# A state space scan turned by phases and scanned in hardware, in place of a tree of complex products

## Chip, cores and metric

The kernel runs on one core of one Trainium2 chip. The metric is the device time of one execution in microseconds (us). Engines: PE (TensorE), DVE (VectorE), ACT (ScalarE), POOL (GpSimd), SP (SyncE). Each engine works through its own instructions in the order in which the program gives them, and waits at the head of its queue for semaphores of the others.

## What is computed

Two transformer blocks on 256 positions of 1024 channels. The second block has a state space branch (S5), an mLSTM branch and a retrieval layer (PEER). The change is in the state space branch alone:

```python
lam = lax.complex(a_re, a_im)
dt = jnp.exp(log_dt)[:, None]
a_bar = jnp.exp(lam * dt)
b_bar = ((a_bar - 1.0) / lam)[..., None] * lax.complex(b_re, b_im)
bu = jnp.einsum('blgc,gpc->blgp', u, b_bar)
a_seq = jnp.broadcast_to(a_bar, (1, L) + a_bar.shape)
def combine(e1, e2):
    a1, b1 = e1
    a2, b2 = e2
    return a1 * a2, a2 * b1 + b2
_, states = lax.associative_scan(combine, (a_seq, bu), axis=1)
y = jnp.real(jnp.einsum('blgp,gcp->blgc', states, c)) + d * u
```

So there is a complex recurrence x[t] = a x[t-1] + bu[t] for each of 32 x 64 states. The kernel takes four positions at a time: with 272 positions there are 68 steps, and the factor of a step is a to the fourth power.

## The kernel before

Weights come through one stream of units of 8 tiles (128x128). For each unit, ACT rounds it into `wh` (line 338), DVE subtracts for the rest `wl` (line 339), and PE does three matmuls for each tile (lines 408 to 410, or 435 to 437 for the z part with 512 columns). Both splits run up to three units ahead of PE (`enter`, line 321); `wh` and `wl` have four buffers each.

All other work is written as generators that `tick` (line 369) steps between units, by a table of costs that each `yield` gives. A scheduler then fixes the order on every engine.

- `_prep` (line 479) runs during the feed forward part of the first block. It computes the step factor on tiles of 16 columns with DVE, and squares it eight times into `pw` (lines 637 to 643): 6 instructions of the helper `cmul` (lines 564 to 569) and one more (line 640) for each square. `expand` (line 503) makes block diagonal matrices on POOL.
- `_block2` (line 668) is the second block up to the retrieval layer. `ssm` (line 746) brings the inputs into `u4` and multiplies them with `ew` into `z2` (real and imaginary part, 16 groups, 68 steps; PE line 769, ACT line 771). Then comes the tree: `step` (line 778) does four DVE instructions for each of six levels up and five or six down, all at line 786. Its reads and writes skip: level i touches every 2, 4, 8, ... steps. Then `py` (lines 809 and 812) takes the states to the output.
- `memory` (line 844) is the mLSTM branch. After a convolution on DVE (line 851) it calls `expand` twice for each of eight column blocks e (lines 862 and 863): one matrix for the keys (buffer e % 2) and one for the values (one buffer). PE multiplies by them: `pk` (line 866) and `pv` (line 873). ACT takes both out of PSUM (lines 867, 875, 876). At the end come the gates: `pg` (line 883), a chain through ACT and DVE over the small tile `GR` (lines 885 to 892), and the matmul `pf` (line 895).
- Meanwhile the main stream of PE is `us`, `xm` (8 units), `z` (8 units), then `g` (16 units); DVE takes each `g` out of PSUM at line 1013, ACT applies tanh at line 1014.

The call that ends the preparation stands at line 1973 (`K.finish(prep)`). `paced` (line 355) makes an instruction be issued after the last product on POOL at line 1951.

Of the kernel before, what the change touches and what calls it, by code (L numbers as in the profile page):

```python
# [14 lines left out]
ALU = mybir.AluOpType  # L15
# [240 lines left out]
def _bc(ap, axis, n):  # L256

    v = ap.unsqueeze(axis)
    shape = list(v.shape)
    shape[axis] = n  # L260
    return v.to_broadcast(shape)
# [217 lines left out]
def _prep(K, dump):  # L479

    nc, I, cols = K.nc, K.I, K.cols
    g = nc.gpsimd
    act, mm, tp = nc.scalar.activation, nc.tensor.matmul, nc.tensor.transpose
    tt, ts, stt = nc.vector.tensor_tensor, nc.vector.tensor_scalar, nc.vector.scalar_tensor_tensor
    EW, CX, TT, ZZ, BX = (K.big(f"s5{i}") for i in range(5))
    ew = EW.a(16, 2, 64)
    cx = [CX.a(16, 4, 16) for _ in range(2)]
    tz = TT.a(16, 64)
    u4 = TT.a(16, 68)
    pw = TT.a(9, 48)  # L490
    z2, tmp = ZZ.a(2, 16, 68), ZZ.a(1088)
    M5 = K.big("ml5")
    mp, nqk = M5.a(513), M5.a(32)
    nc.scalar.dma_start(mp, I["mlp"])
    fold = TT.a(2, 8, 8)
    ex = M5.a(3, P)
    msk = mp[:, 481:513]
    wif = mp[:, 288:480].rearrange("p (a b) -> p a b", b=8)
# [3 lines left out]

        g.tensor_tensor(dst.rearrange("p (a b) -> p a b", b=4), _bc(w[:, 4 * e:4 * e + 4], 1, 32), _bc(msk, 2, 4), ALU.mult)

    K.s5 = ew, cx, tz, z2, tmp, pw, u4
    K.mlf = TT, M5, mp, nqk, wv, fold, ex, expand

    raw = ZZ.t[:, 0:1328]
# [13 lines left out]
        yield 0.1  # L522
    v = [sc[:, i] for i in range(32)]
    dt, rho, th, n, r, sn, cs_, hs, den, kr, ki, u, w = v[:13]
    act(dt, ld, AF.Exp)
    tt(rho, lr, dt, ALU.mult)
    tt(th, li, dt, ALU.mult)
# [11 lines left out]
    act(hs, r, AF.Sin, scale=0.5)  # L539
    tt(hs, hs, hs, ALU.mult)  # L540
    ts(cs_, hs, -2.0, 1.0, ALU.mult, ALU.add)
    ar, ai = pw[:, 8, 0:16], pw[:, 8, 32:48]
    tt(ar, rho, cs_, ALU.mult)
    tt(ai, rho, sn, ALU.mult)
    yield 0.4
# [17 lines left out]
    def cmul(dr, di, xr_, xi, yr, yi, a, b, f):  # L563
        f(a, xr_, yr, ALU.mult)
        f(b, xi, yi, ALU.mult)
        f(dr, a, b, ALU.subtract)
        f(a, xr_, yi, ALU.mult)
        f(b, xi, yr, ALU.mult)
        f(di, a, b, ALU.add)
# [59 lines left out]
    a, b = outputs(), inputs()  # L629
    while True:  # L630
        c, d = next(a, None), next(b, None)
# [1 line left out]
            break  # L633
        yield (c or 0) + (d or 0)

    pr, pi_ = ar, ai
    for i in range(8):
        qr, qi = pw[:, i, 0:16], pw[:, i, 32:48]
        cmul(qr, qi, pr, pi_, pr, pi_, u, w, tt)
        ts(pw[:, i, 16:32], qi, -1.0, None, ALU.mult)  # L640
        pr, pi_ = qr, qi
        if i % 2:
            yield 0.5

    pr4 = ZZ.t[:, 3648:3776]
    v3 = lambda z: z.rearrange("p (e j d) -> p e j d", j=4, d=4)
# [3 lines left out]
    for n in range(10):  # L650
# [8 lines left out]
        v = pf[:, 0:32].rearrange("p (a e b) -> p a e b", a=2, e=2)  # L659
# [8 lines left out]
def _block2(K, X, eps, dump, stop):  # L668
    nc, I, cols = K.nc, K.I, K.cols
    g = nc.gpsimd  # L670
# [1 line left out]
    tt, ts, stt = nc.vector.tensor_tensor, nc.vector.tensor_scalar, nc.vector.scalar_tensor_tensor  # L672
    scopy, vcopy = nc.scalar.copy, nc.vector.tensor_copy
    xr = X[:, :, NM:]
    ew, cx, tz, z2, tmp, pw, u4 = K.s5
    y4 = tmp[:, 0:1024].rearrange("p (a b) -> p a b", a=16)
    TT, M5, mp, nqk, wv, fold, ex, expand = K.mlf

# [67 lines left out]
    def ssm():  # L746

        yield 0.1
        du = K.dram.tile([P, 1088], F32, name="du")
        nc.scalar.dma_start(du, us.rearrange("p n t j -> p (n t j)"))  # L750
        yield 0.1
        d = du.rearrange("(r e c) (n t j) -> e t c n r j", r=4, e=2, n=4, t=4)
        for e in range(2):
            for t in range(4):
                z = 64 * e + 16 * t
                nc.scalar.dma_start(u4[z:z + 16].rearrange("c (n r) j -> c n r j", r=4), d[e, t])
        yield 0.1
        yield 0.1

        for q0 in range(0, 16, 6):  # L760
            ps = []
            for q in range(q0, min(q0 + 6, 16), 3):
                n = min(3, 16 - q)
                p = K.pm_("pe")
                ps.append((q, n, p))
                for j in range(n):
                    for i in range(2):
                        for z in halves:
                            mm(p[z, (i * n + j) * 68:(i * n + j + 1) * 68], ew[z, q + j, i], u4[z, q + j], start=True, stop=True)
            for q, n, p in ps:  # L770
                scopy(z2[:, :, q:q + n], p[:, 0:2 * n * 68].rearrange("p (i a b) -> p i a b", i=2, a=n))
            yield 0.1
        K.bg.sort(key=[sc, ml_, res].index)
        K.e_done = True

        lv = [1, 2, 4, 8, 16, 32]

        def step(i, dst, src):
            z0, zx, z1 = z2[:, :, :, src], z2[:, ::-1, :, src], z2[:, :, :, dst]
            n = z0.shape[3]  # L780
            t = tmp[:, 0:32 * n].rearrange("p (a b c) -> p a b c", a=2, b=16)
            re = _bc(_bc(pw[:, i + 1, 0:16], 1, 2), 3, n)
            im = _bc(pw[:, i + 1, 16:48].rearrange("p (a b) -> p a b", a=2), 3, n)
            c = 0.06 + n * 32 / 960
            for x, y, w, op in ((t, z0, re, ALU.mult), (z1, z1, t, ALU.add), (t, zx, im, ALU.mult), (z1, z1, t, ALU.add)):
                tt(x, y, w, op)  # L786
                spent[0] += c
                if spent[0] > 1.0:
                    yield spent[0]
                    spent[0] = 0.0  # L790

        spent = [0.0]
        N = 68
        for i, d in enumerate(lv):
            m = len(range(2 * d - 1, N, 2 * d))
            if m:
                yield from step(i, slice(2 * d - 1, N, 2 * d), slice(d - 1, d - 1 + 2 * d * (m - 1) + 1, 2 * d))
        for i, d in reversed(list(enumerate(lv))):
            m = len(range(3 * d - 1, N, 2 * d))
            if m:  # L800
                yield from step(i, slice(3 * d - 1, N, 2 * d), slice(2 * d - 1, 2 * d - 1 + 2 * d * (m - 1) + 1, 2 * d))

        for h in range(2):
            p = K.pm_("py")
            for j in range(8):
                q = 8 * h + j
                o = p[:, j * 64:(j + 1) * 64]
                for z in halves:
                    mm(o[z], tz[z, q], u4[z, q, 4:], start=True, stop=False)
                for i in range(2):  # L810
                    for z in halves:
                        mm(o[z], cx[i][z, q].rearrange("p a b -> p (a b)"), z2[z, i, q, 3:67], start=False, stop=i == 1)
            act(y4[:, 8 * h:8 * h + 8], p.rearrange("p (a b) -> p a b", a=8), AF.Gelu_apprx_tanh)
            yield 0.1
        dy = K.dram.tile([P, 1024], F32, name="dy")
        nc.scalar.dma_start(dy, tmp[:, 0:1024])
        yield 0.1
        yt = yv.rearrange("p n (t j) -> p n t j", t=4)
        d = dy.rearrange("(e t c) (n r j) -> r e c n t j", e=2, t=4, n=4, r=4)
        for r in range(4):  # L820
            for e in range(2):
                z = 32 * r + 16 * e
                nc.scalar.dma_start(yt[z:z + 16], d[r, e])
        yield 0.1
        K.R1 = K.big("s5r", F32R)
        K.yh, K.yl = K.R1.a(4, T1), K.R1.a(4, T1)
        K.split(K.yh, K.yl, yv)
        yield 1.1
# [548 lines left out]
def trainium_kernel(ctx, tc, I, O, dump=None, stop=None):  # L1377
# [591 lines left out]
    for i in range(NFF - 3):  # L1969
        up(i)  # L1970
        if i >= DN:
            down(i - DN)
    K.finish(prep)

    with K.behind():
        nc.scalar.dma_start(meta, I["metaT"])
# [57 lines left out]
```

## Time and profile before

| | |
|---|---|
| three runs, median | 1530.45 us (1529.59 to 1530.96) |
| the profiled execution | 1530.96 us; its span 1529.2 us |
| PE busy | 1501.1 us, 98% of the span |
| DVE busy | 1138.1 us, 74% |
| ACT busy | 832.0 us, 54% |
| POOL busy | 237.2 us, 16% |
| granted TensorE clock, mean of the span | 0.995 of full speed |
| second block up to the retrieval layer | about 486 us to 720 us of the span |

Read it like this: PE is busy almost all the time, so other engines matter only where PE waits for them. The list of waits of PE names those places; the timeline of an engine in such a stretch shows what held it up.

### The profile page before, as it was taken

The numbers are of one execution on the slowest core, as the hardware profiler recorded it, in microseconds if no ns is written. First come the engines' busy times: TensorE is split into PE (matmuls) and PEld (weight loads), VectorE is DVE, ScalarE is ACT, GpSimd is POOL, SyncE is SP. The second block draws the span as 40 slices with busy tenths as digits, with TensorE's granted clock in tenths as the row PEclk, the third lists the DMA queues.
The fourth block names the chain that finished last, engine by engine and source line by source line (L and its number), as shares of the span: only waits on it lengthen the run. The fifth ranks groups of instructions, "written<-read, shape, count | busy, mean of one in ns | idle before, by whom it ended". The sixth has DMA issues, their size and how long they took to land.

```text
span 1529.2 us, 30332 instructions
## 1 busy us (share of the span) xinstructions
PE 1501.1 (98%) x11917; PEld 1403.6 (92%) x11917; DVE 1138.1 (74%) x2167; ACT 832.0 (54%) x1442; POOL 237.2 (16%) x257
## 2 busy tenths in 40 slices
PE   8999999999999998999999999999999999999998
PEld 7999899999999987999999999999999888888886
DVE  6865666886867796677989888888998666666664
ACT  7745445775455565665554455555445555555554
POOL 1000000267330020001100522222332000000000
PEclk9999999999999998999999999999999999999999
DMA  7543344555554533446455455554555555555553
GB/s 271 169 136 112 99 150 166 190 197 163 153 179 163 176 114 123 132 159 209 139 184 187 152 177 172 177 160 157 168 165 178 195 193 193 193 193 193 193 194 109
DMA packets 81439, 257.37 MB, mean 168 GB/s; under 512 B 17809, under 2 KB 19601, under 8 KB 81169
## 3 DMA queue, kind: packets, MB, share of 16 engines
q1 hardware_dynamic: 69344, 247.32, 49.2%
q10 hardware_dynamic: 11952, 8.13, 1.7%
q8 instruction: 93, 1.52, 0.4%
q14 instruction: 50, 0.40, 0.1%
HBM read 252.96 MB, written 2.13 MB: 167 GB/s over the span
## 4 chain that ended last, share of the span: by engine, by line
PE 84%; DVE 10%; POOL 2%; issue 2%; ACT 2%; DMA 1%; SPq 0%; ACTq 0%; DVEq 0%; POOLq 0%
PE acc L1340 23%; PE U L408 7%; PE U L410 7%; PE U L409 7%; DVE wl L339 3%; PE g L408 3%; PE g L410 3%; PE g L409 3%; PE u L410 3%; PE u L408 2%; PE u L409 2%; PE pG L1220 2%; DVE s L786 1%; PE acc L1965 1%; PE acc L1963 1%
## 5 line engine op out<-in xcount | busy, mean ns | idle before, releaser
L339 DVE TENSOR_TENSOR wl<-wr,wh 128x1024 fp32r<-128x1024 f32 (+1 forms) x469 | 584.2, 1248 | 196.4 <-ACT wh L338 191.9
L338 ACT CAST wh<-wr 128x1024 fp32r<-128x1024 f32 (+1 forms) x469 | 490.8, 1048 | 387.1 <-PE U L409 144.9
L1340 PE MATMUL acc<-wh,wring 128*128 128x512 f32 x1024 | 315.6, 389 | 0.0
L408 PE MATMUL U<-hh,wh 128*128 128x256 f32 x1024 | 289.8, 283 | 0.0
L410 PE MATMUL U<-hh,wl 128*128 128x256 f32 x1024 | 288.1, 281 | 1.5 <-DVE wl L339 1.4
L409 PE MATMUL U<-hl,wh 128*128 128x256 f32 x1024 | 288.3, 282 | 0.0
L1340 PEld LDWEIGHTS acc<-wh,wring 128*128 128x128 f32 x1024 | 192.2, 188 | 40.0
L1340 PE MATMUL acc<-wl,wring 128*128 128x512 f32 x512 | 199.2, 389 | 0.0
L410 PEld LDWEIGHTS U<-hh,wl 128*128 128x128 f32 x1024 | 193.9, 189 | 1.9 <-DVE wl L339 1.9
L408 PEld LDWEIGHTS U<-hh,wh 128*128 128x128 f32 x1024 | 193.6, 189 | 0.0
L409 PEld LDWEIGHTS U<-hl,wh 128*128 128x128 f32 x1024 | 192.4, 188 | 0.0
L1331 ACT ACTIVATE wring<-act 128x256 fp32r<-128x256 f32 x128 | 53.3, 418 | 149.7 <-PE acc L1340 147.1
L1340 PEld LDWEIGHTS acc<-wl,wring 128*128 128x128 f32 x512 | 96.1, 188 | 19.9
L1301 POOL TENSOR_TENSOR act<-act,ga 128x16 f32<-128x16 f32 (+31 forms) x77 | 74.9, 972 | 191.9 <-ACT ga L1300 170.4
L1332 DVE SCALAR_TENSOR_TENSOR wring<-act,wring 128x256 fp32r<-128x256 f32 x128 | 54.7, 428 | 61.3 <-PE acc L1340 58.9
L410 PE MATMUL u<-hh,wl 128*128 128x256 f32 x320 | 89.9, 282 | 3.3 <-DVE wl L339 3.3
L408 PE MATMUL u<-hh,wh 128*128 128x256 f32 x320 | 90.3, 284 | 0.2 <-ACT hh L440 0.2
L409 PE MATMUL u<-hl,wh 128*128 128x256 f32 x320 | 89.7, 281 | 0.0
L455 POOL TENSOR_TENSOR sq<-sq,sq 128x256 f32<-128x256 f32 x18 | 16.0, 889 | 404.6 <-ACT sq L451 404.4
L408 PE MATMUL g<-hh,wh 128*128 128x256 f32 x256 | 73.7, 288 | 0.0
L409 PE MATMUL g<-hl,wh 128*128 128x256 f32 x256 | 72.0, 281 | 0.0
L410 PE MATMUL g<-hh,wl 128*128 128x256 f32 x256 | 71.9, 281 | 0.0
(639 smaller groups left out, 3309.2 us busy)
## 6 DMA issues: line engine op xcount, KB each, us to landing
wr<-in_W SPq DMA_DIRECT2D x211, 512.0 KB, 3.5
wr<-in_U SPq DMA_DIRECT2D x128, 512.0 KB, 3.8
wr<-in_V SPq DMA_DIRECT2D x128, 512.0 KB, 4.3
tkc<-in_keysT ACTq DMA_DIRECT2D x1, 1024.0 KB, 6.2
wsA<-in_cst ACTq DMA_DIRECT2D x1, 804.0 KB, 6.8
s<-in_s5p ACTq DMA_DIRECT2D x1, 664.0 KB, 4.7
wsA<-in_rows ACTq DMA_DIRECT2D x1, 640.0 KB, 5.5
du<-ml ACTq DMA_DIRECT2D x1, 544.0 KB, 2.7
```

The lines of the kernel that those rows point to most:

```text
L338: a = nc.scalar.copy(hi[:, q], raw[:, q])
L339: b = nc.vector.tensor_tensor(lo[:, q], raw[:, q], hi[:, q].bitcast(F32), ALU.subtract)
L408: mm(out, wh, ah, start=first, stop=False)
L409: mm(out, wh, al, start=False, stop=False)
L410: self.last = mm(out, wl, ah, start=False, stop=last).ins
L455: self.nc.gpsimd.tensor_tensor(self.part[0], self.part[0], s, ALU.add)
L786: tt(x, y, w, op)
L1220: mm(o, r[:, k, :, e % 2], r[:, 4 + 2 * w + k, :, e % 2], start=w == 0, stop=w == 1)
L1301: g.tensor_tensor(d[:, :n], d[:, :n], a[:, :n], ALU.mult)
L1331: act(hi, w, AF.Copy, scale=1.0 / 16384)
L1332: stt(lo, w, 1.0 / 16384, hi.bitcast(F32), ALU.mult, ALU.subtract)
L1340: mm(acc[t][c], w[:, q], v[:, 4 * c:4 * c + 4].rearrange("p a b -> p (a b)"), start=False, stop=i == NE - 1 and len(vs) == 1, skip_group_c ...
```

## The change

Write x[t] = e[t] s[t], where e[t] is the phase of the step factor to the power t (modulus one). Then s obeys a real recurrence, s[t] = r s[t-1] + conj(e[t]) bu[t], with r the modulus of the factor. DVE has an instruction for that (`tensor_tensor_scan`). So the inputs are turned back by their phases, scanned as real and imaginary part, and turned forward again. The table of phases `er`, `ei` (16 groups, 68 steps) is built on POOL by doubling in `phases`, which is called behind the end of the preparation; `r4` holds the modulus for every step, with 0 at the first of a group so that one scan runs over many groups. Groups 0 to 9 are turned on DVE, groups 10 to 15 (`rest`) on POOL.

```diff
-    pw = TT.a(9, 48)
-    z2, tmp = ZZ.a(2, 16, 68), ZZ.a(1088)
+    a1 = TT.a(2, 16)
+
+    er, ei = EW.a(16, 68), CX.a(16, 68)
+    z2, tmp = ZZ.a(2, 16, 68), ZZ.a(1920)
...
+    r4 = TT.a(16, 68)
...
-    pr, pi_ = ar, ai
-    for i in range(8):
-        qr, qi = pw[:, i, 0:16], pw[:, i, 32:48]
-        cmul(qr, qi, pr, pi_, pr, pi_, u, w, tt)
-        ts(pw[:, i, 16:32], qi, -1.0, None, ALU.mult)
-        pr, pi_ = qr, qi
-        if i % 2:
-            yield 0.5
+    cmul(step[0], step[1], cs_, sn, cs_, sn, u, w, tt)
+    cmul(er[:, :, 1], ei[:, :, 1], step[0], step[1], step[0], step[1], u, w, tt)
+    tt(step[2], rho, rho, ALU.mult)
+    tt(step[2], step[2], step[2], ALU.mult)
+    yield 1.5
+
+    def phases():
+        g.memset(er[:, :, 0:1], 1.0)
+        g.memset(ei[:, :, 0:1], 0.0)
+        for m in (1, 2, 4, 8, 16, 32, 64):
+            k = min(m, 67 - m)
+            x = [ZZ.t[:, o:o + 16 * k].rearrange("p (a b) -> p a b", a=16) for o in (1328, 3136)]
+            d, y = slice(m + 1, m + 1 + k), slice(1, 1 + k)
+            cmul(er[:, :, d], ei[:, :, d], er[:, :, y], ei[:, :, y], _bc(er[:, :, m], 2, k), _bc(ei[:, :, m], 2, k), *x, g.tensor_tensor)
+        nc.scalar.copy(r4, _bc(step[2], 2, 68))
+        g.memset(r4[:, :, 0:1], 0.0)
+
+    K.phases = phases
...
-        lv = [1, 2, 4, 8, 16, 32]
-
-        def step(i, dst, src):
-            z0, zx, z1 = z2[:, :, :, src], z2[:, ::-1, :, src], z2[:, :, :, dst]
-            n = z0.shape[3]
-            t = tmp[:, 0:32 * n].rearrange("p (a b c) -> p a b c", a=2, b=16)
-            re = _bc(_bc(pw[:, i + 1, 0:16], 1, 2), 3, n)
-            im = _bc(pw[:, i + 1, 16:48].rearrange("p (a b) -> p a b", a=2), 3, n)
-            c = 0.06 + n * 32 / 960
-            for x, y, w, op in ((t, z0, re, ALU.mult), (z1, z1, t, ALU.add), (t, zx, im, ALU.mult), (z1, z1, t, ALU.add)):
-                tt(x, y, w, op)
...
+        def turn(e, q, j, back, buf):
+            z = z2[:, :, q, j]
+            n, m = z.shape[2], z.shape[3]
+            t = buf[:, :2 * n * m].rearrange("p (a b c) -> p a b c", a=2, b=n)
+            e.tensor_tensor(t, z2[:, ::-1, q, j], _bc(ei[:, q, j], 1, 2), ALU.mult)
+            e.tensor_tensor(z, z, _bc(er[:, q, j], 1, 2), ALU.mult)
+            yield 0.1 + n * m * 4 / 960
+            for i in range(2):
+                e.tensor_tensor(z[:, i], z[:, i], t[:, i], ALU.add if i == back else ALU.subtract)
+            yield 0.1 + n * m * 2 / 960
+
+        def scan(q):
+            flat = lambda z: z[:, q].rearrange("p a b -> p (a b)")
+            for i in range(2):
+                z = flat(z2[:, i])
+                nc.vector.tensor_tensor_scan(z, flat(r4), z, 0.0, ALU.mult, ALU.add)
+                yield 0.1 + z.shape[1] * 2.3 / 960
+
+        all_, out, rest = slice(0, 68), slice(3, 67), slice(10, 16)
+        for _ in turn(g, rest, all_, 0, tmp[:, 1024:]):
+            pass
+        for q in (slice(0, 5), slice(5, 10)):
+            yield from turn(nc.vector, q, all_, 0, tmp)
+        for q in (slice(0, 10), rest):
+            yield from scan(q)
+        for _ in turn(g, rest, out, 1, tmp[:, 1024:]):
+            pass
+        for q in (slice(0, 5), slice(5, 8), slice(8, 10)):
+            yield from turn(nc.vector, q, out, 1, tmp)
...
     K.finish(prep)
+    with K.paced():
+        K.phases()
```

In the changed file the lines behind the edits are shifted: `expand` is line 506 there, the two products of `turn` are lines 794 and 795, its two sums line 798, the scan line 805, and the tanh and the take-out of `g` lines 1031 and 1030.

The order on POOL in the second block, before: the matrices of `expand` (line 503, tile `ml`) stand alone, after two memsets. The first three of the sixteen stand further ahead.

```order
L878 MEMSET GR 128x272 [waits PE_49]
L923 MEMSET ml_6562 128x384 [waits Activation_49,Pool_49]
L503 TENSOR_TENSOR ml_3403<-ml_3403 128x128 [waits PE_49] x3
L503 TENSOR_TENSOR ml_3403<-ml_3403 128x128 [waits PE_49,Pool_49]
L503 TENSOR_TENSOR ml_3403<-ml_3403 128x128 [waits PE_49]
L503 TENSOR_TENSOR ml_3403<-ml_3403 128x128 [waits PE_49,Pool_49]
```

The same place now (`expand` is line 506; the tiles `s` are the states, the phases and the scratch tile):

```order
L895 MEMSET GR 128x272 [waits PE_49]
L940 MEMSET ml_6571 128x384 [waits Activation_49]
L794 TENSOR_TENSOR s_3401<-s_3401,s_3399 128x816 [waits Activation_49,Pool_49]
L795 TENSOR_TENSOR s_3401<-s_3401,s_3398 128x2x408 [waits Pool_49]
L798 TENSOR_TENSOR s_3401<-s_3401 128x408 [waits Pool_49]
L798 TENSOR_TENSOR s_3401<-s_3401 128x408
L506 TENSOR_TENSOR ml_3403<-ml_3403 128x128 [waits PE_49] x3
L506 TENSOR_TENSOR ml_3403<-ml_3403 128x128 [waits PE_49,Pool_49]
L794 TENSOR_TENSOR s_3401<-s_3401,s_3399 128x768 [waits DVE_49]
L795 TENSOR_TENSOR s_3401<-s_3401,s_3398 128x2x6x64 [waits Pool_49]
L506 TENSOR_TENSOR ml_3403<-ml_3403 128x128 [waits PE_49]
L798 TENSOR_TENSOR s_3401<-s_3401 128x6x64 [waits Pool_49]
```

Ahead of the four matrices (values of e = 1, keys of e = 2, values of e = 2, keys of e = 3) now stands the turn back of groups 10 to 15. Ahead of the fifth (values of e = 3) stand the two products of the turn forward, which wait for DVE.

What they wait for on DVE is the last of the four scans (line 805). It stands here, with the splits of the weight stream (line 339) between:

```order
L798 TENSOR_TENSOR s_3401<-s_3401 128x340 x2
L339 TENSOR_TENSOR wl_6657<-wr_6533,wh_6656 128x1024
L805 SCALAR_TENSOR_TENSOR s_3401<-s_3400,s_3401 128x680 x2
L805 SCALAR_TENSOR_TENSOR s_3401<-s_3400,s_3401 128x408
L339 TENSOR_TENSOR wl_6691<-wr_6580,wh_6690 128x1024
L805 SCALAR_TENSOR_TENSOR s_3401<-s_3400,s_3401 128x408
L794 TENSOR_TENSOR s_3401<-s_3401,s_3399 128x640
```

Before, the tree (line 786) stood in this place and reached much further down: its last instruction stood behind line 892, now the last turn on DVE stands ahead of line 888 (905 in the changed file).

On DVE in the preparation, before, the stretch between two splits:

```order
L566 TENSOR_TENSOR s_3400<-s_3400 128x16
L567 TENSOR_TENSOR s_3400<-s_3400 128x16
L568 TENSOR_TENSOR s_3400<-s_3400 128x16
L569 TENSOR_TENSOR s_3400<-s_3400 128x16
L640 TENSOR_SCALAR s_3400<-s_3400 128x16
L1948 SCALAR_TENSOR_TENSOR ffn_3005<-u_4739,cols,ffn_3005 128x255
L1949 SCALAR_TENSOR_TENSOR ffn_3005<-u_4739,cols,ffn_3005 128x254
L339 TENSOR_TENSOR wl_4780<-wr_4590,wh_4779 128x1024
```

and now the same stretch:

```order
L339 TENSOR_TENSOR wl_4742<-wr_4523,wh_4741 128x1024
L661 TENSOR_TENSOR s_3401<-ml_3403 128x128
L662 TENSOR_REDUCE ml_3403<-s_3401 128x32
L1965 SCALAR_TENSOR_TENSOR ffn_3005<-u_4739,cols,ffn_3005 128x255
L1966 SCALAR_TENSOR_TENSOR ffn_3005<-u_4739,cols,ffn_3005 128x254
L339 TENSOR_TENSOR wl_4780<-wr_4590,wh_4779 128x1024
```

The fourteen instructions of two squares that stood ahead of this split are gone; two others have moved up into their place. On PE the order of `pk`, `pv` and the matmuls of the stream between them is the same before and now; `pf` stands 3 matmuls later.

## Rows read from the trace of the kernel before

**Rows 1.** First part of the page: busy time and share of each engine.
```profile
PE 1501.1 (98%) x11917; PEld 1403.6 (92%) x11917; DVE 1138.1 (74%) x2167; ACT 832.0 (54%) x1442; POOL 237.2 (16%) x257
```
**Rows 2.** Waits of PE: who for whom, us in total, times, longest.
```profile
PE pf L895 <- DVE GR L892: 6.7, 1, 6.7
PE u L410 <- DVE wl L339: 3.3, 3, 1.8
...
PE pN L949 <- DVE ml L941: 0.4, 1, 0.4
```
**Rows 3.** Busy time by stretch: each engine (instructions), PE's clock, DMA share, GB/s.
```profile
564.00:579.00 15.00, 15.00 (x131) 12.95 (x129) 14.79 (x16) 7.94 (x17) 0.66 (x1) 1.00 0.32 105
579.00:586.00 7.00, 0.31 (x4) 0.13 (x3) 2.52 (x6) 6.28 (x11) 0.00 (x0) 0.72 0.21 75
586.00:593.00 7.00, 7.00 (x32) 5.96 (x33) 5.25 (x7) 4.67 (x7) 0.00 (x0) 0.55 0.23 77
```
**Rows 4.** Timelines of PE and ACT ahead of `pf`: start, us, [idle before <-releaser].
```profile
571.82 0.62 PE L883 MATMUL pg<-ml,s 128*8 128x272 f32 x2
...
577.30 0.42 ACT L1014 ACTIVATE gs<-gs 128x256 f32<-128x256 f32 x1 [7.06 <-DVE gs L1013]
...
579.25 0.46 ACT L885 ACTIVATE GR<-pg,ml 8x272 f32<-8x272 f32 x1
...
585.96 1.06 PE L895 MATMUL pf<-GR,ml 8*4 8x272 f32 x2 [6.69 <-DVE GR L892]
```
**Rows 5.** Timeline of DVE and PE in the preparation, 394 to 399 us.
```profile
394.20 0.17 DVE L564 TENSOR_TENSOR s<-s 128x16 f32<-128x16 f32 x1
...
396.29 0.17 DVE L640 TENSOR_SCALAR s<-s 128x16 f32<-128x16 f32 x1
...
397.28 1.22 DVE L339 TENSOR_TENSOR wl<-wr,wh 128x1024 fp32r<-128x1024 f32 x1
...
398.56 0.39 PE L410 MATMUL u<-hh,wl 128*128 128x256 f32 x1 [1.80 <-DVE wl L339]
```
**Rows 6.** POOL's free stretch (timeline), and its complex products under load (groups).
```profile
455.41 0.74 POOL L1951 TENSOR_TENSOR ffn<-ffn 128x256 f32<-128x256 f32 x1 [7.98 <-DVE ffn L1949]
502.06 0.33 POOL L878 MEMSET GR<- 128x272 f32 x1 [45.91 <-PE pq L718]
...
L577 POOL TENSOR_TENSOR s<-s,s 128x256 f32<-128x256 f32 x28 | 28.6, 1031 | 1.0
```
**Rows 7.** Timeline of DVE, 530 to 533 us: a start less the one before is a cost.
```profile
530.32 0.43 DVE L834 TENSOR_TENSOR ml<-xm,qq 128x272 f32<-128x272 f32 x1
530.67 0.47 DVE L726 SCALAR_TENSOR_TENSOR X<-X,cols,r2b 128x256 f32<-128x256 f32 x1
531.06 1.21 DVE L339 TENSOR_TENSOR wl<-wr,wh 128x1024 fp32r<-128x1024 f32 x1
532.20 0.49 DVE L851 SCALAR_TENSOR_TENSOR ml<-ml,cols,ml 128x272 f32<-128x272 f32 x1
532.61 1.28 DVE L786 TENSOR_TENSOR s<-s,s 128x1088 f32<-128x1088 f32 x1
```
**Rows 8.** Timeline of DVE: the nearest scan.
```profile
588.63 0.71 DVE L899 TENSOR_TENSOR_SCAN GR<-eye,GR 4x272 f32<-4x272 f32 x1
```
**Rows 9.** Timelines of POOL and DVE where the two meet, at 542 and 867 us.
```profile
542.26 1.46 POOL L503 TENSOR_TENSOR ml<-ml 128x128 f32<-128x128 f32 x1 [0.23 <-PE pv L873]
...
866.59 3.85 POOL L1183 TENSOR_TENSOR tka<-tka,tkc 128x2048 f16<-128x2048 f16 x1 [5.72 <-DVE tka L1182]
...
542.24 1.21 DVE L339 TENSOR_TENSOR wl<-wr,wh 128x1024 fp32r<-128x1024 f32 x1
...
867.29 4.24 DVE L339 TENSOR_TENSOR wl<-wr,wh 128x1024 fp32r<-128x1024 f32 x1
```
**Rows 10.** Timeline of POOL and PE: one matrix of `expand`, and `pv` of e = 3.
```profile
561.17 0.42 POOL L503 TENSOR_TENSOR ml<-ml 128x128 f32<-128x128 f32 x1 [2.73 <-PE pk L866]
...
553.10 0.83 PE L873 MATMUL pv<-ml,ml 128*128 128x128 f32 x6
```

More of the change, by code (lines that the diff above doesn't have):

```diff
@@ L503, in expand @@
         g.tensor_tensor(dst.rearrange("p (a b) -> p a b", b=4), _bc(w[:, 4 * e:4 * e + 4], 1, 32), _bc(msk, 2, 4), ALU.mult)
-    K.s5 = ew, cx, tz, z2, tmp, pw, u4
+    K.s5 = ew, cx, tz, z2, tmp, er, ei, r4, u4
     K.mlf = TT, M5, mp, nqk, wv, fold, ex, expand
@@ L524, in _prep @@
     dt, rho, th, n, r, sn, cs_, hs, den, kr, ki, u, w = v[:13]
+    step = v[13:17]
     act(dt, ld, AF.Exp)
@@ L541, in _prep @@
     ts(cs_, hs, -2.0, 1.0, ALU.mult, ALU.add)
-    ar, ai = pw[:, 8, 0:16], pw[:, 8, 32:48]
+    ar, ai = a1[:, 0], a1[:, 1]
     tt(ar, rho, cs_, ALU.mult)
@@ L674, in _block2 @@
     xr = X[:, :, NM:]
-    ew, cx, tz, z2, tmp, pw, u4 = K.s5
+    ew, cx, tz, z2, tmp, er, ei, r4, u4 = K.s5
     y4 = tmp[:, 0:1024].rearrange("p (a b) -> p a b", a=16)
@@ L774, in ssm @@
         K.e_done = True
-        lv = [1, 2, 4, 8, 16, 32]
-        def step(i, dst, src):
-            z0, zx, z1 = z2[:, :, :, src], z2[:, ::-1, :, src], z2[:, :, :, dst]
-            n = z0.shape[3]
-            t = tmp[:, 0:32 * n].rearrange("p (a b c) -> p a b c", a=2, b=16)
-            re = _bc(_bc(pw[:, i + 1, 0:16], 1, 2), 3, n)
-            im = _bc(pw[:, i + 1, 16:48].rearrange("p (a b) -> p a b", a=2), 3, n)
-            c = 0.06 + n * 32 / 960
-            for x, y, w, op in ((t, z0, re, ALU.mult), (z1, z1, t, ALU.add), (t, zx, im, ALU.mult), (z1, z1, t, ALU.add)):
-                tt(x, y, w, op)
[L787 to L801, printed above, removed]
+        def turn(e, q, j, back, buf):
[8 more added lines that the diff above has]
+            yield 0.1 + n * m * 2 / 960
```

## The prediction, made before the changed kernel ran

> **What bounds the kernel now.** The first view is the page's table of busy times: PE is busy for 98% of the span, DVE for 74% [rows 1]. A DVE instruction that disappears is therefore worth nothing by itself; only time in which PE stands still, or runs at the lower clock, can be won or lost. The second view, the waits of PE, names such places. The reader is to see that two entries have to do with this change: one long wait of 6.7 us at `pf`, and three short ones of 3.3 us together for a split of the weights [rows 2]. The third view, busy time by stretch, shows what the long wait costs on top: behind it the granted clock is 0.55 in a stretch of 7 us, which is the lower level (1.2 GHz) for most of it, and 7 x 0.45 = 3.1 us of work are lost; I use 3.0 [rows 3]. Ahead of it DVE is busy 14.8 of 15 us [rows 3]: the tree is what holds the chain up. The fourth view, the timelines ahead of `pf`, shows how: `pg` ended at 572.4, but ACT stood 7.1 us behind a tanh that waited for DVE, and so began line 885 only at 579.25, just when PE arrived at `pf` (585.96 less 6.69). PE then waited for the whole chain up to line 892 [rows 4].
>
> **The change, part by part.**
>
> *Squares in the preparation.* PE waits 1.80 us for the split at 397.28. Ahead of it stand fourteen instructions on 16 columns, from 394.20 to 396.4, 2.2 us [rows 5]. They are gone, and two small ones have moved in (about 0.5 us). So 1.7 of the 1.8 us go, and of the next wait, under another square, about 0.5. I take -2.2; bounds -3.0 (all three short waits) and 0 (another wait ends last).
>
> *The phase table on POOL.* 42 products and sums, six each of 16, 32, 64, 128, 256, 512 and 48 columns. POOL's price is 0.42 us for 128 columns [rows 10] and 3.85 us for 2048 [rows 9], so 0.19 us and 1.79 ns a column; the 42 make 19.4 us. Under DVE's load the 256-column products took 1.03 us [rows 6] against 0.65 by that price, so up to 31 us. POOL is free from 456.2 for 45.9 us [rows 6], so the table ends near 487 and is hidden. If the cover is too short, it falls on the opening of the second block at 486: bounds 0 and +4, taken 0. The copy into `r4` is one ACT instruction, and ACT is busy 54% [rows 1]: 0.
>
> *The new wait.* POOL's fifth matrix of the group (values of e = 3) now stands behind two products that wait for DVE's last scan, and PE, in order, cannot pass `pv` of e = 3, which ran at 553.10 [rows 10]. When is that scan done? DVE's work is the same as before up to 530.67 [rows 7]. Behind it now stand, ahead of the end of the fourth scan: 6 splits at 1.14 us, 9 of line 851 at 0.41, 2 of line 834 at 0.35, one of line 726 at 0.39 (all from differences of starts, [rows 7]): 11.6 us. The tree's 1088 columns take 1.21 us (1.28 less the 0.07 by which rows overlap) [rows 7]: 1.06 ns a column. So four turns of 680 columns take 0.78 and four of 340 take 0.42: 4.8 us. The scan in the trace takes 0.64 us net for 272 columns [rows 8], 2.13 ns a column and 0.06 us: two of 680 at 1.51 and two of 408 at 0.93, 4.9 us. That is 21.3 us, and the end would be at 552.0.
>
> But the trace shows that DVE and POOL shut each other out. A split that takes 1.14 us alone took 4.24 us when a POOL instruction of 3.85 us had begun 0.7 us earlier, and a POOL matrix of 0.42 us took 1.46 when a split had begun just before it [rows 9, 10]. POOL's turn back (two of 816 columns at 1.65, two of 408 at 0.92: 5.1 us) and four matrices (1.7 us) fall into this time and DVE has almost no gap: the scans end near 558.5 (0.3 us of this overlaps line 834, which reads PSUM). Then POOL does 768 columns (1.56), DVE 640 (0.74), POOL 768 (1.56), DVE again (0.74), and the matrix (0.42): `pv` can start at 563.5. That is **+10.4 us**. The bounds: +2.3 if the two engines do not block each other (552.0 + 3.1 + 0.4 = 555.5), +12.7 if a split gets in ahead of each of POOL's last two products. The first bound goes against rows 9, so I stay nearer the second. What waits behind: PE's whole stream, but nothing else, because ACT and DVE have splits ahead. Earlier short waits of PE (`pk` of e = 2, behind an ACT instruction that now waits longer for line 851) are swallowed by this one. The clock falls as it does behind 6.7 us of idling: **+3.0** [rows 3]; bounds 0 and 3.1.
>
> POOL's price rests on a 2-byte row for the long end. The Trainium skill's page GPSIMD Engine Reference, section Performance versus the Vector engine, gives 4497 ns for a two-input add of 2048 4-byte elements, 2.2 ns each. By that, an estimate, the 3984 columns ahead of the matrix would take 1.2 us longer than by my price, and the sum would be +4.0 in place of +2.8.
>
> *The old wait.* The tree's last instructions no longer stand between ACT's tanh and its input. Line 885 can follow the end of `pg` at once, in place of 6.9 us later [rows 4]. PE needs about 7 us from `pg` to `pf` (572.4 to 579.27 before, 3 matmuls more now), the chain 6.7 us (579.25 to 585.96), and it starts at most about 0.8 us behind `pg` [rows 4]. So 0.5 us of waiting is left, and the low clock behind it goes: -6.7 - 3.0 + 0.5 = **-9.2**; bounds -9.7 (no wait left) and -6.7 (the low clock comes all the same).
>
> *Behind it.* `pf`, the transposes and `pN` follow each other faster now, with the same chain through ACT and DVE. One such place cost 0.4 us before [rows 2]. I take two of that size, +0.8; bounds 0 and +3, half of the old chain. The tree's 44 instructions on DVE and the 24 that replace them (8 of the turn back, 4 scans, 12 of the turn forward) cost nothing else: PE's own work covers them.
>
> **Sum:** -2.2 + 0 + 10.4 + 3.0 - 9.2 + 0.8 = +2.8 us on the profiled execution of 1530.96 us, so **1533.8 us**. That execution is 0.5 us above the median of 1530.45. About 0.2%, 3 us, is what a measurement of this kernel can tell from no change.
>
> **Rivals.** *B, faster: the new wait is short.* One mechanism: DVE's two-input instructions and POOL overlap, the last scan ends at 552.0 and `pv` waits 2.3 us, too short for the clock to fall. Then -2.2 + 2.3 - 9.2 + 0.8 = -8.3: 1522.7 us. It decides from the point where the new wait is below about 7 us. For it: single small DVE instructions beside POOL grew by little. Against it: the 4.24 us split [rows 9]. The Trainium skill's page SBUF — State Buffer, section Who interferes with whom, says that a DVE instruction with two SBUF inputs and a GpSimd instruction that reads SBUF lock each other out for the whole instruction. By that rule, which the 4.24 us row bears out, B falls.
>
> *C, slower: the table is not hidden.* If POOL is still at the 512-column level when the second block opens at 486, the eight DVE instructions that make the first operands there wait up to 1.1 us each, and PE behind them: +4, 1537.8 us. For it: 31 us is an estimate from a load like that. Against it: 15 us are left to 502.
>
> *D, the change of place only:* the new wait comes out near 7 us and the gains eat it: about 1530.5 us, no change.
>
> **How the numbers follow.** Forecast 0.55, B 0.20, C 0.15, D 0.10. The forecast's own range is 1530 to 1537 by its bounds; two thirds of it lie more than 3 us above the median, nearly all of the rest within. Faster: 0.20 from B and 0.01, 0.21. Same: 0.18 from the forecast and 0.09 from D, 0.27. Slower: 0.36 + 0.15 + 0.01 = 0.52. The range that leaves out the shorter half of B and the worst of C is 1525 to 1539.
>
> **What would show it.** In the waits of PE of the changed kernel: an entry at `pv` (line 890 there) for the matrix on POOL, 7 to 11 us, and none over 1 us at `pf`. In POOL's timeline: the two 768-column products directly ahead of that matrix, begun at the end of the fourth scan. In the stretches: a low clock behind that wait. In the preparation: no wait of 1.8 us. The prediction is wrong if `pv` waits under 7 us (then faster), if the wait at `pf` stays, or if PE waits between 484 and 500 us while POOL still builds the table.

## The result, and the profile after

| | before | changed |
|---|---|---|
| median of 4 runs, us | 1530.7 | 1547.04 |
| lowest to highest, us | 1529.59 to 1532.22 | 1544.27 to 1548.81 |
| ratio to before, 95% interval | 1 | 1.0106 [1.0094, 1.0119] |
| profiled execution, us (span) | 1530.96 (1529.2) | 1548.81 (1547.0) |

The changed kernel is 16.3 us slower by the medians. 1533.8 was forecast, with a range that ended at 1539. The sign was right, the size was not. The profiled execution is the slowest of its four, 17.85 us above the profiled one of before.

The page's table of busy times answers to [rows 1]:

```profile
PE 1506.5 (97%) x11917; PEld 1406.8 (91%) x11917; DVE 1133.9 (73%) x2105; ACT 834.0 (54%) x1444; POOL 280.2 (18%) x310
```

PE has as many instructions as before, and DVE, with 62 fewer, has only 4.2 us less to do. POOL got the 43 us that the table and its part of the turn take there. What the change did to the time stands, as before, in the waits of PE. This view answers to [rows 2]:

```profile
PE pv L890 <- POOL ml L506: 12.4, 1, 12.4
PE g L410 <- DVE wl L339: 3.5, 2, 2.6
PE acc L1981 <- DVE ffnr L441: 1.8, 1, 1.8
...
PE pt L994 <- ACT ml L989: 1.3, 1, 1.3
...
PE pf L912 <- DVE GR L909: 0.7, 1, 0.7
```

The 6.7 us at `pf` have become 0.7, and there is one long wait at `pv`. Both were forecast, the wait at `pv` with 10.4 us. The entries at `acc` and `pt` are new, the one at `g` was 0.3 us before, and of the three the prediction's sum has only 0.8 us for what comes behind `pf`. The next view gives busy time by stretch, with the columns of [rows 3]; the first two numbers are the stretch's length and PE's busy time in it:

```profile
482.00:485.00 3.00, 0.97 (x6) 0.57 (x5) 2.80 (x3) 1.35 (x2) 2.84 (x4) 1.00 0.12 46
485.00:490.00 5.00, 5.00 (x32) 5.00 (x31) 3.81 (x6) 2.41 (x5) 0.97 (x4) 0.66 0.65 208
550.00:557.00 7.00, 5.98 (x27) 4.09 (x25) 7.00 (x8) 6.41 (x14) 0.00 (x0) 1.00 0.58 194
557.00:569.00 12.00, 0.00 (x0) 0.00 (x0) 11.97 (x10) 0.83 (x2) 9.24 (x6) 0.66 0.25 90
569.00:575.00 6.00, 5.72 (x18) 4.83 (x19) 1.29 (x2) 0.52 (x2) 1.32 (x3) 0.55 0.26 87
...
635.00:640.00 5.00, 2.46 (x21) 2.26 (x20) 2.73 (x8) 1.37 (x5) 0.00 (x0) 1.00 0.00 0
640.00:645.00 5.00, 3.60 (x26) 3.06 (x26) 1.89 (x4) 4.94 (x9) 0.00 (x0) 1.00 0.36 107
645.00:653.00 8.00, 7.08 (x32) 6.32 (x32) 7.29 (x14) 6.34 (x14) 0.00 (x0) 0.57 0.40 124
```

Below, what PE **loses** in a stretch is its idle time plus its busy time multiplied by (1 less the granted clock). From these rows: at 482 to 490, 2.03 + 5.00 x 0.34 = 3.7 us; around `pv`, 1.0 + 12.0 + 0.3 + 5.72 x 0.45 = 15.9; at 635 to 653, 2.5 + 1.4 + 0.9 + 7.08 x 0.43 = 7.9. In each the low clock stands behind idle time of PE. The ledger against the profiled execution of before, from the same view taken over both spans microsecond by microsecond:

| place | lost before | lost after | difference |
|---|---|---|---|
| preparation, 394 to 403 | 2.8 | 0.5 | -2.3 |
| end of the first block, 482 to 490 | 0 | 3.7 | +3.7 |
| `pv`, 550 to 575 | 0 | 15.9 | +15.9 |
| `pf` (579 to 593 before, 598 to 602 after) | 9.9 | 0.8 | -9.1 |
| memory's norm (635 to 640 before, 635 to 653 after) | 0.8 | 7.9 | +7.1 |

That is +15.3 of 17.85 us. Another 0.8 is a short idle time at 44 us, far ahead of anything that the change touches; the last 1.7 us are not found in one place. Of the 7.9 us at the memory's norm 4.9 are idle time and 3.0 the low clock behind it. The second part doesn't come every time: in the profiled executions of `e1_turn_on_dve` and `e3_table_left_out`, below, the same place loses 5.1 us, all of it idle time, at the full clock.

**The wait at `pv`.** The timelines of POOL and DVE ahead of it, and of PE:

```profile
534.32 2.78 POOL L794 TENSOR_TENSOR s<-s,s 128x816 f32<-128x816 f32 x1 [29.37 <-ACT s L785]
...
543.81 0.43 POOL L506 TENSOR_TENSOR ml<-ml 128x128 f32<-128x128 f32 x1 [1.72 <-PE pk L883]
544.48 0.40 POOL L506 TENSOR_TENSOR ml<-ml 128x128 f32<-128x128 f32 x1 [0.24 <-PE pv L890]
...
559.68 2.33 POOL L794 TENSOR_TENSOR s<-s,s 128x768 f32<-128x768 f32 x1 [10.15 <-DVE s L805]
562.08 2.29 POOL L795 TENSOR_TENSOR s<-s,s 128x768 f32<-128x768 f32 x1
564.34 1.40 POOL L506 TENSOR_TENSOR ml<-ml 128x128 f32<-128x128 f32 x1
565.70 2.19 POOL L798 TENSOR_TENSOR s<-s 128x384 f32<-128x384 f32 x2
567.84 2.08 POOL L506 TENSOR_TENSOR ml<-ml 128x128 f32<-128x128 f32 x2
...
558.60 0.99 DVE L805 TENSOR_TENSOR_SCAN s<-s,s 128x408 f32<-128x408 f32 x1
...
569.28 1.65 PE L890 MATMUL pv<-ml,ml 128*128 128x128 f32 x6 [12.37 <-POOL ml L506]
```

The fourth scan ended at 559.6 (558.5 forecast), POOL's two products took 2.3 us each (1.56 forecast), and PE did not go on behind the next matrix, at 565.7, but only once the sums and the matrix behind them were done, at 569.3. So the matrix of the values of e = 3 is the sixth of its group and not the fifth, as the section on the change and the prediction said: two sums and one matrix more stood ahead of it. The first lines show why. The first matrix of the group waits for a `pk`, so it is one for the keys (e = 2), and the second waits for a `pv`, so it is one for the values (e = 1). Keys come first in each pair, and the order is keys 2, values 1, keys 3, values 2, keys 4, values 3.

### The profile page after: what moved, and what is told of

Same layout as the page of the kernel before. It is cut to its first block, busy times and chain, and to the rows that moved or that the text cites. A ratio compares the mean times of both kernels' runs of the same rounds, so it can differ in the third digit from the quotient of the medians.

```text
span 1547.0 us, 30314 instructions
## 1 busy us (share of the span) xinstructions
PE 1506.5 (97%) x11917; PEld 1406.8 (91%) x11917; DVE 1133.9 (73%) x2105; ACT 834.0 (54%) x1444; POOL 280.2 (18%) x310
## 4 chain that ended last, share of the span: by engine, by line
PE 82%; DVE 9%; ACT 3%; POOL 2%; issue 1%; DMA 1%; ACTq 0%; SPq 0%; DVEq 0%; POOLq 0%
PE acc L1357 23%; PE U L408 6%; PE U L410 6%; PE U L409 6%; DVE wl L339 3%; PE g L408 3%; PE g L410 3%; PE g L409 3%; PE u L410 2%; PE u L408 2%; PE u L409 2%; PE pG L1237 2%; PE acc L1982 1%; PE acc L1980 1%; PE acc L1981 1%
## 5 line engine op out<-in xcount | busy, mean ns | idle before, releaser
L339 DVE TENSOR_TENSOR wl<-wr,wh 128x1024 fp32r<-128x1024 f32 (+1 forms) x469 | 590.4, 1261 | 208.6 <-ACT wh L338 205.5
```

What stands on the lines that cost most here:

```text
L339: b = nc.vector.tensor_tensor(lo[:, q], raw[:, q], hi[:, q].bitcast(F32), ALU.subtract)
```

## Experiments

Four kernels first, each with one edit of the changed kernel. Two places that the prediction did not see had to be tested too: 482 and 637. One word needs care: the recorded expectations call the second of the two edits below, the turn behind the scans, the turn back, and the first the turn forward. The section on the change and the text here have it the other way round: back ahead of the scans, forward behind them.

**The turn on DVE.** The edit of `e1_turn_on_dve`:

```diff
-        for _ in turn(g, rest, all_, 0, tmp[:, 1024:]):
+        for _ in turn(nc.vector, rest, all_, 0, tmp[:, 1024:]):
...
-        for _ in turn(g, rest, out, 1, tmp[:, 1024:]):
+        for _ in turn(nc.vector, rest, out, 1, tmp[:, 1024:]):
```

> The whole turn, forward and back, on DVE; POOL keeps the phase table and the matrices. Theory (POOL's share of the turn stands ahead of the matrices, and POOL and DVE lock each other out): the wait of 12.4 us at pv and the 3.8 us lost to the low clock around it go; DVE does 5 us more but loses no time to POOL, so the wait at pf stays under 2 us: 1530 to 1533 us against 1547.0. Rival (DVE's scans are too late anyway, the wait only changes its place): over 5 us of waiting at pf, 1537 to 1542 us. Second rival (the lock-out costs little): 2 to 3 us slower than the kernel that moves the turn back alone.

Measured: 1535.34 us (8 runs, 1533.49 to 1537.73), ratio to before 1.0028 [1.0018, 1.0039]. `e2_back_on_dve` makes the second of the two edits alone (the turn forward):

> Only the turn back of the six states (two products of 768 columns, two sums of 384) moves from POOL to DVE; nothing else changes its place in any engine's order. Theory (these four instructions stand ahead of the matrix of the values of e = 3 on POOL): the wait at pv falls from 12.4 us to under 1, DVE has 2.7 us more to do: 1531 to 1534 us. Rival (the scan itself is late because POOL's turn forward locks DVE out): the wait comes back at pf with over 4 us: 1537 to 1541 us.

Measured: 1536.92 us (5 runs), ratio 1.0043 [1.0029, 1.0058]. With four instructions moved from POOL to DVE, and nothing else, 10.1 us of the 16.3 are gone and so is the 12.4 us wait at `pv`: these four, in their place ahead of the matrix on POOL, caused it. With the turn back on DVE too it is another 1.6 us less, where the second rival wanted 2 to 3 more; but the two intervals overlap, so the runs do not price the lock-out between DVE and POOL in the turn back.

Both results lie above the theory's range, and yet there is no long wait at `pf`. The longest wait of PE in `e2_back_on_dve`, from the view of its waits:

```profile
PE g L408 <- ACT ml L1021: 4.9, 1, 4.9
```

and ACT's timeline there:

```profile
572.94 2.42 ACT L1021 ACTIVATE ml<-z,rr 128x512 f32<-128x512 f32 x4 [7.40 <-DVE s L795]
```

This is a wait that neither theory named. The tanh of line 1021 fills `hz`, which lies in the buffer `ml3`. PE goes on with the next `g` only when that tanh has emptied a bank of PSUM. And the tanh waits for DVE's line 795, a product of the turn forward that has nothing to do with its data. What they share is a buffer: the change put the phases' real parts, `er`, into `EW`, whose other content (`ew`) is read for the last time at the states' matmuls; `ml3` takes over the place of `EW`; and `er` is read up to the last turn forward. Before, the same line (L1004 there) began at 548.23 and waited for nothing but PE:

```profile
548.23 1.37 ACT L1004 ACTIVATE ml<-z,rr 128x512 f32<-128x512 f32 x2 [1.28 <-PE z L437]
```

In the changed kernel it began at 582.70, without a cost of its own, as PE had been idle for 12 us by then.

**The buffer.** `e5_swap` starts from `e1_turn_on_dve` and lets two tables change places:

```diff
-    er, ei = EW.a(16, 68), CX.a(16, 68)
+    r4, ei = EW.a(16, 68), CX.a(16, 68)
...
-    r4 = TT.a(16, 68)
+    er = TT.a(16, 68)
```

> The whole turn on DVE as in e1_turn_on_dve, and the two tables change places: the phases' real parts lie where the decays lay (in TT, which lives to the end), the decays in EW, whose place the buffer of the memory's gates (ml3) takes. Theory (the wait of 4.5 us at the first g there is ACT's tanh that must not write into ml3 before the turn back has read its last phase; the decays are read for the last time at the fourth scan, some 12 us earlier): the wait and the low clock behind it, 6.9 us together, go: 1528 to 1530 us against 1535.3. Rival (ACT is behind DVE at that point whatever the buffer): the wait stays or comes back at pf with over 3 us, 1533 to 1536 us.

Measured: 1531.09 us, median of 10 runs from 1527.03 to 1533.53, ratio 1.0006 [0.9996, 1.0015]; the profiled execution, 1529.07, lies in the theory's range, the median 1 us above it. The wait is gone. ACT's timeline shows the tanh 13 us earlier than in `e1_turn_on_dve` (571.26 there), right behind the fourth scan, as the theory had it:

```profile
558.45 1.26 ACT L1021 ACTIVATE ml<-z,rr 128x512 f32<-128x512 f32 x2 [6.75 <-DVE s L805]
```

By the medians that is 4.3 us, by the profiled executions 7.0. Why this kernel's runs spread more than the others' stays open.

**The table.** `e3_table_left_out` fills the table with ones:

```diff
-            cmul(er[:, :, d], ei[:, :, d], er[:, :, y], ei[:, :, y], _bc(er[:, :, m], 2, k), _bc(ei[:, :, m], 2, k), *x, g.tensor_tensor)
+            for z in (er, ei):
+                g.memset(z[:, :, d], 1.0)
```

> The phase table is left out: POOL fills it with ones by 12 memsets in place of 42 products and sums, so the states are not turned by their true phases; every other engine's order stays. Theory (POOL's products slow DVE's splits between 455 and 486 us until PE waits at 482): the wait of 1.8 us and the low clock behind it go, 3.7 us less: 1543 us; everything behind it, the 12.4 us at pv too, stays as it is. Rival (the place is late for another reason, or the products do not slow DVE): 1547 us, the wait stays.

Measured: 1541.49 us (1539.96 to 1542.18), ratio 1.0072 [1.0056, 1.0089]: 5.5 us less than the change. The wait at 482 is gone, the one at `pv` is 12.4 us as before: the theory holds. Beyond its 3.7 us another 1.4 come from the stretch behind 496, where the changed kernel (as the one before) loses 2.4 us and this one 1.05, without a low clock; that this too is the table's doing is not shown. The mechanism is plain in DVE's splits of the weights. First the changed kernel, then `e3_table_left_out`:

```profile
474.68 1.62 DVE L339 TENSOR_TENSOR wl<-wr,wh 128x1024 fp32r<-128x1024 f32 x1 [0.39 <-ACT wh L338]
477.52 2.17 DVE L339 TENSOR_TENSOR wl<-wr,wh 128x1024 fp32r<-128x1024 f32 x1
481.88 2.30 DVE L339 TENSOR_TENSOR wl<-wr,wh 128x1024 fp32r<-128x1024 f32 x1
```

```profile
473.67 1.23 DVE L339 TENSOR_TENSOR wl<-wr,wh 128x1024 fp32r<-128x1024 f32 x1 [1.29 <-ACT wh L338]
476.51 1.23 DVE L339 TENSOR_TENSOR wl<-wr,wh 128x1024 fp32r<-128x1024 f32 x1 [0.51 <-ACT wh L338]
479.38 1.23 DVE L339 TENSOR_TENSOR wl<-wr,wh 128x1024 fp32r<-128x1024 f32 x1 [0.20 <-ACT wh L338]
```

Beside POOL's products of 512 columns a split takes up to 2.30 us in place of 1.23, and the last pieces of the feed-forward have no lead to give.

Can the table stand elsewhere? `e6_early` emits it in pieces from the end of the preparation on, between POOL's products of the feed-forward; `phases` becomes a generator that yields behind each piece:

```diff
-            cmul(er[:, :, d], ei[:, :, d], er[:, :, y], ei[:, :, y], _bc(er[:, :, m], 2, k), _bc(ei[:, :, m], 2, k), *x, g.tensor_tensor)
+            ops = []
+            cmul(er[:, :, d], ei[:, :, d], er[:, :, y], ei[:, :, y], _bc(er[:, :, m], 2, k), _bc(ei[:, :, m], 2, k), *x, lambda *z: ops.append(z))
+            for o in range(0, 6, 6 if m < 16 else 3):
+                with K.paced():
+                    for z in ops[o:o + (6 if m < 16 else 3)]:
+                        g.tensor_tensor(*z)
+                yield 0.1
...
-    yield 0.1
+    yield from phases()
```

> The phase table's 42 instructions on POOL in eight pieces from the end of the preparation on, between POOL's products of the feed-forward, in place of all behind the last of them. Theory (its products slow DVE most at the end of the first block, where the last pieces of the feed-forward have no lead): the table ends about 15 us earlier, the wait of 1.8 us at 482 and the low clock behind it go as where the table was left out: 1541.5 to 1543.5 us against 1547.0. Rival (POOL's products of the feed-forward now stand behind the table and PE waits for them instead): 1546 us or more, with waits of PE between 430 and 460 us.

Measured: 1546.77 us (1544.12 to 1550.04), ratio 1.0100 [1.0084, 1.0115]: no gain, as the rival had it. The loss at 482 is gone, and 3.6 us are lost at 453 to 460 instead. In `e7_all`, below, where the table stands the same, the timelines of POOL and ACT show why:

```profile
441.45 2.81 POOL L658 TENSOR_TENSOR s<-s 128x64 f32<-128x64 f32 x4
444.34 1.88 POOL L658 TENSOR_TENSOR s<-s,s 128x128 f32<-128x128 f32 x2
446.29 0.46 POOL L658 TENSOR_TENSOR s<-s 128x128 f32<-128x128 f32 x1
446.71 0.74 POOL L1972 TENSOR_TENSOR ffn<-ffn 128x256 f32<-128x256 f32 x1
...
443.21 1.05 ACT L338 CAST wh<-wr 128x1024 fp32r<-128x1024 f32 x1 [1.14 <-PE acc L1985]
447.49 0.41 ACT L440 CAST ffnr<-ffn 128x256 fp32r<-128x256 f32 x1 [3.23 <-POOL ffn L1972]
```

Eighteen instructions of the table, from 435.8 to 446.7, stand ahead of that product of the feed-forward. ACT's cast of the result waits 3.23 us for it, ACT's casts of weights stand behind that, DVE's splits and sums behind those, and PE waited 1.9 us at `pm`. In `e6_early` itself the same cast waits 3.22 us and `pm` 1.9.

**The order behind.** What happens at 635 to 653? ACT's timeline of the changed kernel:

```profile
622.81 1.03 ACT L338 CAST wh<-wr 128x1024 fp32r<-128x1024 f32 x1
...
627.06 5.43 ACTq L840 DMA_DIRECT2D ml<-dy  x7
632.53 0.23 ACT L974 ACTIVATE ssq<-pN 128x1 f32<-128x1 f32 x2 [5.07 <-DMA ml<-dy]
632.65 0.42 ACT L1031 ACTIVATE ml<-ml 128x256 f32<-128x256 f32 x1
632.96 1.05 ACT L338 CAST wh<-wr 128x1024 fp32r<-128x1024 f32 x1
```

Seven of the eight transfers that bring the scan's output back are issued one behind the other, 0.78 us each in the mean, and ACT does nothing for 5.07 us; between two casts of weights lie 10 us. Before, the longest row of them was four, issued behind work that ACT already had, and cost it 2.14 us. They moved because the order is made by pacing: the generator of the scan has other steps than that of the tree, and so falls elsewhere beside the memory's. `e4_two_ticks` puts two empty steps behind the last turn forward (`yield from [0.1] * 2`), which brings the transfers to the place that they had beside the memory's norm:

> Two empty steps of the pacing behind the turn back, so that the scan's output comes two places later in the order of all engines, in the same place beside the memory's instructions as in the kernel before. Theory (between 636 and 655 us the new order costs PE 8.2 us against 0.7 before, because splits stand behind the memory's norm and ACT issues eight transfers with nothing queued ahead): the loss there falls to under 2 us: 1539 to 1542 us. Rival (it is late because everything since pv is late, whatever the order): no change, 1546 to 1548 us.

Measured: 1540.07 us (1539.57 to 1540.70), ratio 1.0061 [1.0044, 1.0078]: 7.0 us less than the change. In that stretch 0.7 us are lost in place of 7.9. The theory holds and the rival falls: everything ahead of it, the 12.4 us at `pv` too, is as late as in the change. `e8_issue_on_pool` leaves the pacing and issues the eight transfers elsewhere:

```diff
-                nc.scalar.dma_start(yt[z:z + 16], d[r, e])
+                nc.gpsimd.dma_start(yt[z:z + 16], d[r, e])
```

> Only the eight transfers that bring the scan's output back are issued by POOL, which is idle there, in place of ACT; the pacing is that of the change. Theory (the 5 us in which ACT's queue issues them without a break make its casts of the weights late, and that costs the 7.7 us between 637 and 653): the loss there falls under 2 us, 1540 to 1542 us. Rival (the place beside the memory's norm is what costs, whoever issues): the waits for g there stay, 1545 us or more.

Measured: 1538.88 us (1537.45 to 1541.03), ratio 1.0058 [1.0043, 1.0073]: 8.2 us less, and no loss at that place. The theory holds. One thing is not separated: either edit also changes the order of ACT's and DVE's instructions around the place, so the runs show that the issuing on ACT at that place costs the time, not how much of it is ACT standing still and how much is the order that was built around that. The Trainium skill's page Perfetto Trace Analysis, section What "DMA-bound" means, says that a solid row of transfers on the issuing engine's own track is descriptor generation and no movement of data. The row of 5.43 us on ACT's queue is of that kind; what fills it this trace doesn't show.

**All together.** `e7_all` has the turn on DVE, the two tables changed over, the early table and the two empty steps:

> All four together: the turn on DVE, the two tables changed over, the table early, two empty steps behind the turn back. If the four losses are separate, as the runs so far show (11.6 us by the turn, 6.9 by the buffer, 3.7 to 5.5 by the table, 5 to 7 by the order): 1517 to 1521 us, 10 to 13 below the kernel before. If DVE or ACT bound the memory's chain in another way, a wait comes back at pf: 1524 to 1528 us.

Measured: 1524.24 us (1522.99 to 1524.89), ratio 0.9958 [0.9945, 0.9972]: faster than before, but 3 us above the range, and not by a wait at `pf`. What is left over is the 3.6 us of the early table. `e9_small_pieces` cuts the table finer:

```diff
-            for o in range(0, 6, 6 if m < 16 else 3):
+            for o in range(0, 6, 3 if m < 16 else 2):
```

> As e7_all, with the table in pieces of three instructions in place of six, and of two in place of three for the large ones, so that 9 and not 18 of them stand between two of POOL's products of the feed-forward. Theory (in e7_all the product of the last piece but one came 3 us late behind the table, ACT's casts behind it, and PE waited 1.9 us at pm and lost 1.7 us to the low clock): that loss goes and the table still ends by 476, ahead of the old place of waiting at 482: 1520 to 1521.5 us against 1524.2. Rival (wherever the table stands, POOL's products slow the splits until PE waits once): a wait of about 2 us at either place, 1523.5 us or more.

Measured: **1520.26 us** (5 runs, 1519.32 to 1520.72), ratio 0.9930 [0.9916, 0.9943]: the best of all, 10.3 us below the kernel before and 26.8 below the change. Busy time by stretch, for `e7_all` and then for `e9_small_pieces`, around the place and, last, around the old one at 482:

```profile
452.00:454.00 2.00, 0.10 (x1) 0.10 (x1) 2.00 (x4) 1.98 (x3) 1.84 (x3) 1.00 0.35 139
454.00:459.00 5.00, 5.00 (x30) 5.00 (x31) 2.16 (x3) 0.64 (x2) 4.92 (x5) 0.66 0.59 210
```

```profile
452.00:459.00 7.00, 7.00 (x60) 6.99 (x60) 5.04 (x7) 5.09 (x7) 6.20 (x8) 1.00 0.47 150
478.00:488.00 10.00, 10.00 (x84) 9.83 (x83) 8.70 (x17) 7.80 (x15) 0.00 (x0) 1.00 0.50 161
```

PE is busy throughout at both places, at the full clock. The same table, on the same engine, costs 3.6 us or nothing by how many of its instructions stand between two that others wait for. `e10_pieces_and_pool` replaces the empty steps by the issuing on POOL:

> As e9_small_pieces, but in place of the two empty steps the eight transfers of the scan's output are issued by POOL. Theory (ACT's issuing was the cause of the loss behind 637, so either cure gives the same): within 1.5 us of e9_small_pieces, no loss over 1 us between 620 and 650. Rival (the empty steps also help elsewhere): 3 us or more above it.

Measured: 1521.43 us (4 runs, 1518.85 to 1524.57), ratio 0.9932 [0.9917, 0.9947]. Within 1.2 us of `e9_small_pieces`, with no loss behind 620, so either cure does. Its profiled execution, the slowest of the four, shows another wait, told in the last section.

## Why the prediction came out as it did

1. *Squares in the preparation*, -2.2: measured -2.3. Right by the ledger; no run tests it alone.
2. *The phase table*, 0, with bounds of 0 and +4: measured +3.7. The end of the table was met (486.1, forecast near 487), but "hidden" was wrong, and rival C had the price right with the wrong mechanism: no operand of the second block came late. The table slowed DVE's splits while it ran, and PE waited in the last pieces of the feed-forward. The prediction used the lock-out of [rows 9] to price the wait at `pv` and forgot it for the 29 us that POOL is busy between 455 and 486 beside the same splits. A cover is no cover if it shares the resource.
3. *The new wait at `pv`*, +10.4 and +3.0 for the clock behind it: measured 12.4, and 15.9 with the small waits next to it and the clock. Mechanism, place and releaser are right; the size fell 2.5 us short. `pv` ran at 569.3, and 563.5 was forecast: 1.1 us because the last scan ended later, 1.1 because the two products and the matrix behind them took 6.1 us on POOL in place of 5.0, and 3.5 because the matrix is the sixth and not the fifth of its group, with two sums and a matrix more ahead of it. Of this, 2.2 us cost nothing here: by 523 us PE itself was that much later than before. So it is partly luck that the end of the scans was only 1.1 us off: counted from there, their stretch was 1.1 us shorter than forecast. That the matrix is the sixth could have been read from the order, which has one matrix between the products and the sums and two behind, by counting which `pk` and `pv` frees the place of each. Rival B fell with it, and the clock that it took for such a wait isn't borne out: it held 2.3 us to be too short for the clock to fall, but at 482 to 485 PE stood idle for 2.0 us and the clock behind was 0.66.
4. *The old wait at `pf`*, -9.2: measured -9.1. In the change alone that proves little, as PE came 12 us later; in `e5_swap` and `e9_small_pieces`, where PE does not wait at `pv`, `pf` waits 0.7 us too. Right.
5. *Behind it*, +0.8, with bounds of 0 and +3: measured +7.1. **This step failed most**, by 6.3 of the 15 us by which the forecast missed the profiled execution (it missed the median by 13.2). It priced the chain behind `pf` as if the rest of the order stayed. But the same edit replaced the steps by which the order is paced, and the eight transfers came to a place where ACT had no work queued ahead of them. `e4_two_ticks` and `e8_issue_on_pool` give 7.0 and 8.2 us back.
6. *Not in the list at all*: the buffer. It cost nothing in the change, where the wait at `pv` hid it, but 4.5 to 4.9 us and the clock behind as soon as that wait was gone. The order of the changed kernel gave it away: the tanh of line 1021 waits there for DVE and POOL, and before only for PE.

So terms 1 and 4 stood, and 3 in its mechanism; 2 and 5, both taken at next to nothing, are 10.0 us, and the size of 3 another 2.5, of the 15 us between forecast and profiled execution.

## What to carry to other kernels

Work on an idle engine is hidden only if nothing that it shares (a port, a queue, a place in the order) belongs to an engine that has no slack, so check each added stretch against what runs beside it and not against when it ends. When a tensor is put into the spare part of an existing buffer, the buffer lives as long as its longest reader: look up who takes its place next. And where yields or estimated times make the order, rewriting one generator moves its neighbours: compare the order behind the edit too, transfers that are issued by a computing engine first.

## What the runs showed of the hardware

The lock-out between DVE and POOL is harsher for the short instruction than the prediction's rows had it. In the profiled execution of `e10_pieces_and_pool` PE waited 3.0 us at `pv` for a matrix of 128 columns, which stood behind another that took long. The view of line 506 gives the shortest, median and longest of the sixteen, in ns:

```profile
L506 POOL TENSOR_TENSOR ml<-ml x16: 393/466/5419, 291.4 to 569.1; 128x128 f32<-128x128 f32 x16
```

5.4 us in place of 0.4, from 542.9 to 548.3, while DVE went from one two-input instruction to the next without a gap. In `e9_small_pieces` at the same place the longest was 1.4 us. The Trainium skill's page SBUF — State Buffer, section Who interferes with whom, says that the ports that the two share are an exclusive lock, and that the order of issue decides who blocks. A matrix that stands still for 5.0 us beside DVE's instructions agrees with a lock, and it outlasted several of them running: a split, two sums, another split and a scan. So a scan seems to hold the ports too: one on 680 columns, 1.56 us from 546.55, lies wholly within that time, and the matrix ended 0.2 us behind it. That the time of such a matrix varies so may be why `e10_pieces_and_pool` spread over 5.7 us; this was not tried.
